# Two products of a chunked state-space scan, done in three rounded passes instead of one in full precision, with the carried state updated in place

## The chip, the cores and the metric

One core of a Trainium2 chip. The time is the device time of one execution in microseconds (us); of several runs the median is given.

## The reference

A decoder layer on 512 tokens of 1024 channels in float32: a gated feed-forward block, a mixer with two parallel branches (sliding-window attention and a Mamba-2 scan), and a second feed-forward block, each with a layer norm behind it. The change touches the scan. It goes over 4 groups of 8 heads and, in each, over 4 chunks of 128 tokens:

```
CB = jnp.einsum("bclgn,bcsgn->bcgls", Cc, Bc)
y_diag = jnp.einsum("bcgls,bcgkls,bcsgkp->bclgkp", CB, Lmat, xdt)
decay_states = jnp.exp(A_cum[..., -1:] - A_cum)
states = jnp.einsum("bclgn,bcgkl,bclgkp->bcgkpn", Bc, decay_states, xdt)
...
    return d_c[..., None, None] * h + s_c, h
...
y_off = jnp.einsum("bclgn,bcgkpn,bcgkl->bclgkp", Cc, prev, jnp.exp(A_cum))
```

`states` is the state that a chunk adds, `prev` the state carried into a chunk, and `y_off` what the carried state gives to the output.

## The kernel before

Everything is one Tile program; each engine gets its instructions in one fixed order, which a scheduler lays down ahead of time from the program's priorities and from when it expects operands to be ready. So a changed instruction also changes the order of its neighbours, on every engine.

Large products use float32 weights and activations that are split into a rounded high part and a rounded low part (`F32R`). `mm3` (L123 to L126) makes one product of two such pairs in three passes: high by high, high by low, low by high. `split_w` (L96 to L102) splits a weight block of 128x1024: ScalarE (ACT) writes the high part `wh` (L99), VectorE (DVE) subtracts it from the raw block to get `wl` (L100). `split_act` (L142 to L146) does the same for activations (L144 on ACT, L145 on DVE). A product of two plain `F32` operands is one call of `nc.tensor.matmul`; in the trace it has two records.

The scan is `ssd(g)`, a generator, for groups g = 0 to 3. For each chunk c, `lead` builds `ud` on GpSimd (POOL, L572), `decays` multiplies `ud` by a triangle on TensorE (PE, L583, L584), takes `exp` on ACT (`seg`, L586), makes `cb` (L589, L591), multiplies `seg` by it on DVE (L593), and prepares `xdt` (DVE, L595), `yx` (POOL, L597) and, for the first three chunks, `xds` = `xdt` times its decay (POOL, L601). `products` multiplies `seg` by `xdt` (L609, eight matmuls of 64 columns, two records each), then for c > 0 the carried product `CT` by `prev` (L615), and for c < 3 the state product `Bn` by `xds` (L621). DVE scales and adds the results; the new `prev` is the old one times its decay (POOL, L626) plus the state product (L627), written to the other of two buffers. After that `yx` is gated (L629), squared on ACT (L632), scaled by `rs` (DVE L633, POOL L634, DVE L635), and `turn` transposes it on PE (L642) and splits it into `uT`.

These steps are woven into the large products by `weave`: after each main step (24 passes of 512 columns on PE) it lets the generator do one step more. The mains are the input projections `z_tiles` and `conv_tile` of the next group and the output products `w_ssm_tiles` of the group before; in the last weave, `gs_tile`, whose gate `tg` and operand `m1` have one buffer each in the pool `sp`, and whose loads and stores POOL issues. The tile pool `wp` holds three raw weight blocks and four split ones; the PSUM tiles `sm` number four.

Of the kernel before, what the change touches and what calls it, by code (L numbers as in the profile page):

```python
# [9 lines left out]
F32 = mybir.dt.float32  # L10
F32R = mybir.dt.float32r
# [3 lines left out]
P = 128  # L15
# [24 lines left out]
def hybrid_layer(  # L40
# [18 lines left out]
    def sm(name="sm"):  # L59
        return psum.tile([P, 512], F32, tag="sm", name=name)  # L60
# [62 lines left out]
    def mm3(ps, lh, ll, rh, rl, start, stop):  # L123
        nc.tensor.matmul(ps, lh, rh, start=start, stop=False)  # L124
        nc.tensor.matmul(ps, lh, rl, start=False, stop=False)  # L125
        cur["mm"] = nc.tensor.matmul(ps, ll, rh, start=False, stop=stop)  # L126
# [15 lines left out]
    def split_act(dst, ps):  # L142

        a = nc.scalar.copy(dst[0], ps)  # L144
        b = nc.vector.tensor_tensor(dst[1], ps, f(dst[0]), ALU.subtract)  # L145
        return a.ins, b.ins  # L146
# [141 lines left out]
    with tc.tile_pool(name="mix", bufs=1) as mix:  # L288
# [258 lines left out]
        with tc.tile_pool(name="ssd", bufs=1) as sp:  # L547
            ysum = sp.tile([P, 8, SEQ], F32, name="ysum")

            def ssd(g):  # L550
                uT = sp.tile([P, 4, 2, SEQ], F32R, name="uT", bufs=1)
                cst["u", g] = uT
                xn, BT, CT, Bn = cst["x", g], cst["B", g], cst["C", g], cst["Bn", g]
                hs = slice(g * HPG, (g + 1) * HPG)
                normB = sp.tile([P, 512], F32, name="normB", bufs=1)
                nc.gpsimd.dma_start(normB, norm_w[0, g * 512:(g + 1) * 512].partition_broadcast(P))

                def hb(ap):
                    return ap.unsqueeze(2).broadcast_to([P, HPG, HD])

                def hv(ap):
                    return ap.rearrange("p (h d) -> p h d", h=HPG)

                st = [{} for _ in range(NT)]

                def lead(c):
                    st[c]["ud"] = []
                    for q4 in range(2):
                        ud = sp.tile([P, 2, 4, P], F32R, name="ud", bufs=2)
                        h0 = g * HPG + 4 * q4  # L570
                        for i in range(2):
                            nc.gpsimd.tensor_tensor(  # L572
                                ud[:, i], upper.unsqueeze(1).broadcast_to([P, 4, P]),
                                f(dAr[:, i, c, h0:h0 + 4]).unsqueeze(2).broadcast_to([P, 4, P]), ALU.mult)
                        st[c]["ud"].append(ud)

                def decays(c):
                    tok = slice(c * P, (c + 1) * P)
                    segs = []
                    for ud in st[c]["ud"]:  # L580
                        ps = sm()
                        udv = ud.rearrange("p i h l -> p i (h l)")
                        nc.tensor.matmul(ps, lower_r, udv[:, 0], start=True, stop=False)  # L583
                        nc.tensor.matmul(ps, lower_r, udv[:, 1], start=False, stop=True)  # L584
                        seg = sp.tile([P, 4, P], F32, name="seg", bufs=4)
                        nc.scalar.activation(seg.rearrange("p h l -> p (h l)"), ps, AF.Exp)  # L586
                        segs.append(seg)
                    pcb = sm()
                    nc.tensor.matmul(pcb[:, :P], BT[:, tok], CT[:, tok], start=True, stop=True)  # L589
                    cb = sp.tile([P, P], F32, name="cb", bufs=2)  # L590
                    nc.vector.tensor_tensor(cb, pcb[:, :P], quarter, ALU.mult)  # L591
                    for seg in segs:
                        nc.vector.tensor_tensor(seg, seg, cb.unsqueeze(1).broadcast_to([P, 4, P]), ALU.mult)  # L593
                    xdt = sp.tile([P, 512], F32, name="xdt", bufs=2)
                    nc.vector.tensor_tensor(hv(xdt), hv(xn[:, c]), hb(dth[:, c, hs]), ALU.mult)  # L595
                    yx = sp.tile([P, 512], F32, name="yx", bufs=2)
                    nc.gpsimd.tensor_tensor(hv(yx), hv(xn[:, c]), hb(dB[:, hs]), ALU.mult)  # L597
                    xds = None
                    if c + 1 < NT:
                        xds = sp.tile([P, 512], F32, name="xds", bufs=1)  # L600
                        nc.gpsimd.tensor_tensor(hv(xds), hv(xdt), hb(dec[:, 1, c, hs]), ALU.mult)  # L601
                    st[c].update(segs=segs, xdt=xdt, yx=yx, xds=xds)

                def products(c):
                    tok = slice(c * P, (c + 1) * P)
                    segs, xdt, yx, xds = (st[c][k] for k in ("segs", "xdt", "yx", "xds"))
                    py = sm()
                    for h in range(HPG):
                        nc.tensor.matmul(py[:, h * HD:(h + 1) * HD], segs[h // 4][:, h % 4], xdt[:, h * HD:(h + 1) * HD],  # L609
                                         start=True, stop=True)  # L610
                    nc.vector.tensor_tensor(yx, yx, py, ALU.add)
                    if c > 0:
                        prev = st[c]["prev"]
                        po = sm()
                        nc.tensor.matmul(po, CT[:, tok], prev, start=True, stop=True)  # L615
                        yo = sp.tile([P, 512], F32, name="yo", bufs=1)
                        nc.vector.tensor_tensor(hv(yo), hv(po), hb(dec[:, 0, c, hs]), ALU.mult)
                        nc.vector.tensor_tensor(yx, yx, yo, ALU.add)
                    if c + 1 < NT:
                        pst = sm()  # L620
                        nc.tensor.matmul(pst, Bn[:, c], xds, start=True, stop=True)  # L621
                        new = sp.tile([P, 512], F32, name="prev", bufs=2)
                        if c == 0:
                            nc.vector.tensor_copy(new, pst)
                        else:
                            nc.gpsimd.tensor_tensor(hv(new), hv(prev), hb(dec[:, 2, c, hs]), ALU.mult)  # L626
                            nc.vector.tensor_tensor(new, new, pst, ALU.add)  # L627
                        st[c + 1]["prev"] = new
                    nc.vector.tensor_tensor(yx, yx, cst.pop(("z", g, c)), ALU.mult)  # L629
                    rs = sp.tile([P, P], F32, name="rs", bufs=2)  # L630
                    sq = sp.tile([P, 512], F32, name="yo", bufs=1)
                    nc.scalar.activation(sq, yx, AF.Square, accum_out=rs[:, 0:1])  # L632
                    nc.vector.tensor_scalar(rs[:, 0:1], rs[:, 0:1], 1.0 / 512.0, 4.0 * RMS_EPS, ALU.mult, ALU.add)  # L633
                    nc.gpsimd.tensor_tensor(rs[:, 1:2], rs[:, 0:1], mhalf[:, 0:1], ALU.pow)  # L634
                    nc.vector.scalar_tensor_tensor(yx, yx, rs[:, 1:2], normB, ALU.mult, ALU.mult)  # L635

                def turn(c):
                    tok = slice(c * P, (c + 1) * P)
                    yx = st[c]["yx"]
                    ps = sm()  # L640
                    for i in range(4):
                        nc.tensor.transpose(ps[:, i * P:(i + 1) * P], yx[:, i * P:(i + 1) * P], ident)  # L642
                    split_act((uT[:, :, 0, tok], uT[:, :, 1, tok]), ps.rearrange("p (i t) -> p i t", i=4))

                lead(0)
                yield
                for c in range(NT + 1):
                    if c < NT:
                        decays(c)
                        yield  # L650
                    if c > 0:
                        turn(c - 1)
                    if c < NT:
                        products(c)
                        if c + 1 < NT:
                            lead(c + 1)
                        yield
# [15 lines left out]

            def gs_tile(j):
                ps = gemm_T(load_w(wcols(w_in, 0, 8, OFF_GS + j * P, P)), xT, range(8))
                tg = sp.tile([P, SEQ], F32, name="tg", bufs=1)
                nc.scalar.activation(tg, ps, AF.Tanh, scale=0.5)
                nc.gpsimd.dma_start(gsd[j], tg)
                m1 = sp.tile([P, SEQ], F32, name="m1", bufs=1)
                nc.gpsimd.dma_start(m1, m1d[j])  # L680
                nc.vector.scalar_tensor_tensor(ysum[:, j], tg, 1.0, ysum[:, j], ALU.add, ALU.mult)
                nc.vector.tensor_tensor(ysum[:, j], ysum[:, j], m1, ALU.add)
# [54 lines left out]
```

## Time and profile before

| what | value |
|---|---|
| median of 3 runs | 1452.49 us (1450.7 to 1454.38) |
| the profiled execution | 1453.2 us, span of its trace 1451.5 us |
| mean granted TensorE clock | 0.994 |
| PE busy | 1426.5 us, 98% of the span |
| weight loads (PEld) | 1169.7 us, 81% |
| DVE busy | 791.5 us, 55% |
| ACT busy | 482.1 us, 33% |
| POOL busy | 195.3 us, 13% |
| DMA | 106 GB/s mean over the span |

A share of busy time is a mean over stages with different loads. PE's matmuls are pipelined, so that the record of one overlaps the next one's; what a matmul holds of PE is read from the distance between records. In a line of the timeline the number in brackets is the engine's idle time just before it, and what ended it.

### The profile page before, as it was taken

What the parts mean: (1) busy time and instruction counts of PE and PEld (TensorE: products, weight loads), DVE (VectorE), ACT (ScalarE), POOL (GpSimd) and SP (SyncE); (2) the same over time, 40 slices, a digit from 0 to 9 for tenths busy, and PEclk for the clock granted to TensorE, in tenths of its full rate; (3) what the DMA queues carried; (4) which work ended last, traced back from release to release, by engine and by line L of the source; (5) the groups of instructions that cost most, each with busy time, mean ns of one, the idle gap of its engine ahead of it and who ended that gap; (6) DMA issues with size and microseconds to landing.
All of it is one profiled execution on the core that took longest, in us unless ns stands there. A gap on an engine that the chain in (4) does not pass through costs nothing. (4 is left out here: it accounts for less than half of the span.)

```text
span 1451.5 us, 17121 instructions
## 1 busy us (share of the span) xinstructions
PE 1426.5 (98%) x6700; PEld 1169.7 (81%) x6700; DVE 791.5 (55%) x1246; ACT 482.1 (33%) x789; POOL 195.3 (13%) x214
## 2 busy tenths in 40 slices
PE   8999999999999999999999999999999999999997
PEld 6888888888877777887888888878878888888885
DVE  4343343233867884358659588686574434433235
ACT  4232232121346775223444234223313322322220
POOL 1000000000000000245244154261110000000001
PEclk9999999999999999999999999999999999999999
DMA  8433333323422133641231322345735333333321
GB/s 273 121 88 102 98 90 102 99 89 105 138 81 72 45 86 108 199 119 56 80 87 59 95 73 74 95 124 161 222 110 181 95 102 95 95 102 93 97 87 58
DMA packets 195633, 154.46 MB, mean 106 GB/s; under 512 B 6532, under 2 KB 169424, under 8 KB 195552
## 3 DMA queue, kind: packets, MB, share of 16 engines
q1 hardware_dynamic: 188608, 130.17, 30.1%
q0 software_dynamic: 6944, 23.19, 5.0%
q8 instruction: 53, 0.87, 0.3%
q14 instruction: 28, 0.23, 0.0%
HBM read 140.76 MB, written 12.58 MB: 106 GB/s over the span
## 5 line engine op out<-in xcount | busy, mean ns | idle before, releaser
L100 DVE TENSOR_TENSOR wl<-raw,wh 128x1024 fp32r<-128x1024 f32 (+1 forms) x233 | 299.6, 1287 | 417.3 <-ACT wh L99 412.6
L99 ACT CAST wh<-raw 128x1024 fp32r<-128x1024 f32 (+1 forms) x233 | 244.3, 1050 | 694.4 <-issue 323.7
L124 PE MATMUL acc<-xT,wh 128*128 128x512 f32 (+2 forms) x1120 | 441.9, 395 | 0.0
L125 PE MATMUL acc<-xT,wh 128*128 128x512 f32 (+2 forms) x1120 | 434.8, 388 | 0.0
L126 PE MATMUL acc<-xT,wl 128*128 128x512 f32 (+2 forms) x1120 | 433.8, 387 | 0.0
L124 PEld LDWEIGHTS acc<-xT,wh 128*128 128x128 f32 x1120 | 210.9, 188 | 44.5 <-issue 3.2
L125 PEld LDWEIGHTS acc<-xT,wh 128*128 128x128 f32 x1120 | 210.7, 188 | 44.2 <-issue 3.3
L126 PEld LDWEIGHTS acc<-xT,wl 128*128 128x128 f32 x1120 | 210.4, 188 | 43.0 <-issue 0.2
L124 PE MATMUL dn<-wh,hT 128*128 128x512 f32 x352 | 137.2, 390 | 0.0
L125 PE MATMUL dn<-wl,hT 128*128 128x512 f32 x352 | 137.1, 390 | 0.0
L126 PE MATMUL dn<-wh,hT 128*128 128x512 f32 x352 | 136.9, 389 | 0.0
L160 POOL TENSOR_TENSOR sts<-sts,cols 128x1 f32<-128x1 f32 x12 | 11.9, 990 | 719.9 <-DVE sts L159 719.9
L572 POOL TENSOR_TENSOR ud<-upper,dAr 128x512 fp32r<-128x512 f32 x64 | 86.4, 1378 | 104.2 <-PE sm L584 104.2
L239 DVE TENSOR_TENSOR t<-t,acc 128x512 f32<-128x512 f32 x44 | 30.2, 687 | 111.6 <-PE acc L126 111.4
L125 PEld LDWEIGHTS dn<-wl,hT 128*128 128x128 f32 x352 | 66.1, 188 | 13.7
L126 PEld LDWEIGHTS dn<-wh,hT 128*128 128x128 f32 x352 | 66.1, 188 | 13.6
L124 PEld LDWEIGHTS dn<-wh,hT 128*128 128x128 f32 x352 | 66.1, 188 | 13.6
L124 PE MATMUL z<-wh,xT 128*128 128x512 f32 x128 | 51.5, 402 | 0.0
L124 PE MATMUL acc<-uT,wh 128*128 128x512 f32 x128 | 50.5, 395 | 0.0
L126 PE MATMUL z<-wh,xT 128*128 128x512 f32 x128 | 49.9, 390 | 0.0
L125 PE MATMUL z<-wl,xT 128*128 128x512 f32 x128 | 49.9, 390 | 0.0
L126 PE MATMUL acc<-uT,wl 128*128 128x512 f32 x128 | 49.9, 390 | 0.0
(212 smaller groups left out, 1691.8 us busy)
## 6 DMA issues: line engine op xcount, KB each, us to landing
raw<-in_w_in_dram SPq DMA_DIRECT2D x66, 512.0 KB, 3.7
raw<-in_ffn_w_gate_dram SPq DMA_DIRECT2D x44, 512.0 KB, 3.8
raw<-in_ffn_w_up_dram SPq DMA_DIRECT2D x44, 512.0 KB, 3.7
raw<-in_ffn_w_down_dram SPq DMA_DIRECT2D x44, 512.0 KB, 3.6
raw<-in_w_ssm_branch_dram SPq DMA_DIRECT2D x16, 512.0 KB, 3.4
raw<-in_w_attn_branch_dram SPq DMA_DIRECT2D x8, 512.0 KB, 4.1
raw<-in_w_out_dram SPq DMA_DIRECT2D x8, 512.0 KB, 4.4
r<-in_x_dram SPq DMA_DIRECT2D x8, 256.0 KB, 5.7
```

Source lines behind the costliest of these rows:

```text
L99: nc.scalar.copy(h[:, :n], raw[:, :n])
L100: nc.vector.tensor_tensor(l[:, :n], raw[:, :n], f(h[:, :n]), ALU.subtract)
L124: nc.tensor.matmul(ps, lh, rh, start=start, stop=False)
L125: nc.tensor.matmul(ps, lh, rl, start=False, stop=False)
L126: cur["mm"] = nc.tensor.matmul(ps, ll, rh, start=False, stop=stop)
L160: nc.gpsimd.tensor_tensor(mv[:, 3:4], mv[:, 2:3], mhalf[:, 0:1], ALU.pow)
L239: nc.vector.tensor_tensor(t, t, pu, ALU.mult)
L572: nc.gpsimd.tensor_tensor(ud[:, i], upper.unsqueeze(1).broadcast_to([P, 4, P]), f(dAr[:, i, c, h0:h0 + 4]).unsqueeze(2).broadcast_to([P, 4 ...
```

## The change

The carried state `prev` and the decayed inputs (now `xd`) are each split into a high and a low part (`prs`, `xds`), and so are `C` and `B` of the chunk (`csp`, `bsp`); the two products go through `mm3`. There is one buffer of `prev` for the group, and POOL's multiply and DVE's addition write it in place. The splits of `C`, `B` and `xd` are in `decays`, that of `prev` in `products`. To make room, `gs_tile` takes its two tiles from the pool `mix`, under the names `th` (two buffers) and `ct` (three buffers), which the conv tiles use too.

```diff
+                    if c > 0:
+                        csp = sp.tile([P, 2, P], F32R, name="csp", bufs=1)
+                        split_act((csp[:, 0], csp[:, 1]), CT[:, tok])
+                        st[c]["csp"] = csp
                     if c + 1 < NT:
-                        xds = sp.tile([P, 512], F32, name="xds", bufs=1)
-                        nc.gpsimd.tensor_tensor(hv(xds), hv(xdt), hb(dec[:, 1, c, hs]), ALU.mult)
+                        xd = sp.tile([P, 512], F32, name="xd", bufs=1)
+                        nc.gpsimd.tensor_tensor(hv(xd), hv(xdt), hb(dec[:, 1, c, hs]), ALU.mult)
+                        bsp = sp.tile([P, 2, P], F32R, name="bsp", bufs=1)
+                        split_act((bsp[:, 0], bsp[:, 1]), Bn[:, c])
+                        xds = sp.tile([P, 2, 512], F32R, name="xds", bufs=1)
+                        split_act((xds[:, 0], xds[:, 1]), xd)
+                        st[c]["bsp"] = bsp
...
-                        nc.tensor.matmul(po, CT[:, tok], prev, start=True, stop=True)
+                        mm3(po, csp[:, 0], csp[:, 1], prs[:, 0], prs[:, 1], True, True)
...
-                        nc.tensor.matmul(pst, Bn[:, c], xds, start=True, stop=True)
-                        new = sp.tile([P, 512], F32, name="prev", bufs=2)
+                        mm3(pst, bsp[:, 0], bsp[:, 1], xds[:, 0], xds[:, 1], True, True)
                         if c == 0:
-                            nc.vector.tensor_copy(new, pst)
+                            prev.append(sp.tile([P, 512], F32, name="prev", bufs=1))
+                            nc.vector.tensor_copy(prev[0], pst)
                         else:
-                            nc.gpsimd.tensor_tensor(hv(new), hv(prev), hb(dec[:, 2, c, hs]), ALU.mult)
-                            nc.vector.tensor_tensor(new, new, pst, ALU.add)
-                        st[c + 1]["prev"] = new
+                            nc.gpsimd.tensor_tensor(hv(prev[0]), hv(prev[0]), hb(dec[:, 2, c, hs]), ALU.mult)
+                            nc.vector.tensor_tensor(prev[0], prev[0], pst, ALU.add)
+                        prs = sp.tile([P, 2, 512], F32R, name="prs", bufs=1)
+                        split_act((prs[:, 0], prs[:, 1]), prev[0])
+                        st[c + 1]["prs"] = prs
...
-                tg = sp.tile([P, SEQ], F32, name="tg", bufs=1)
+                tg = mix.tile([P, SEQ], F32, name="th", bufs=2)
...
-                m1 = sp.tile([P, SEQ], F32, name="m1", bufs=1)
+                m1 = mix.tile([P, SEQ], F32, name="ct", bufs=3)
```

The order of PE hardly moves; where it does, it is by a few passes. Of DVE, group 1, chunk 2, from the sum `yx`+`yo` on, before:

```order
L618 TENSOR_TENSOR yx<-yx,yo 128x512
L595 TENSOR_TENSOR xdt<-xn,dth 128x512
L629 TENSOR_TENSOR yx<-yx,zs 128x512
L100 TENSOR_TENSOR wl<-raw,wh 128x1024
L633 TENSOR_SCALAR rs<-rs 128x1
L305 SCALAR_TENSOR_TENSOR ct<-acc,cols,ct 128x511
L635 SCALAR_TENSOR_TENSOR yx<-yx,rs,normB 128x512
L305 SCALAR_TENSOR_TENSOR ct<-acc,cols,ct 128x510
```

The same place in the changed kernel (its lines are numbered up to 13 higher):

```order
L628 TENSOR_TENSOR yx<-yx,yo 128x512
L145 TENSOR_TENSOR prs<-prev,prs 128x512
L642 TENSOR_TENSOR yx<-yx,zs 128x512
L145 TENSOR_TENSOR csp<-CT,csp 128x128
L145 TENSOR_TENSOR bsp<-Bn,bsp 128x128
L145 TENSOR_TENSOR xds<-xd,xds 128x512
L305 SCALAR_TENSOR_TENSOR ct<-acc,cols,ct 128x511
L646 TENSOR_SCALAR rs<-rs 128x1
L596 TENSOR_TENSOR xdt<-xn,dth 128x512
L648 SCALAR_TENSOR_TENSOR yx<-yx,rs,normB 128x512
L305 SCALAR_TENSOR_TENSOR ct<-acc,cols,ct 128x510
L100 TENSOR_TENSOR wl<-raw,wh 128x1024
```

Four subtractions have come in ahead of the second `seg` multiply of the chunk, and one weight subtraction has moved behind the scaling of `yx`.

Of DVE, group 0, chunk 1, from the scaling of chunk 0's `yx` to the second `seg`, before:

```order
L635 SCALAR_TENSOR_TENSOR yx<-yx,rs,normB 128x512
L100 TENSOR_TENSOR wl<-raw,wh 128x1024
L305 SCALAR_TENSOR_TENSOR ct<-acc,cols,ct 128x511
L591 TENSOR_TENSOR cb<-sm,quarter 128x128
L305 SCALAR_TENSOR_TENSOR ct<-acc,cols,ct 128x510
L593 TENSOR_TENSOR seg<-seg,cb 128x512
```

and in the changed kernel:

```order
L145 TENSOR_TENSOR bsp<-Bn,bsp 128x128
L145 TENSOR_TENSOR xds<-xd,xds 128x512
L648 SCALAR_TENSOR_TENSOR yx<-yx,rs,normB 128x512
L305 SCALAR_TENSOR_TENSOR ct<-acc,cols,ct 128x511
L592 TENSOR_TENSOR cb<-sm,quarter 128x128
L305 SCALAR_TENSOR_TENSOR ct<-acc,cols,ct 128x510
L594 TENSOR_TENSOR seg<-seg,cb 128x512
```

The weight subtraction between `yx` and `cb` has moved away, behind this chunk, and two new subtractions stand ahead of `yx`.

Of POOL, group 0, from `yx` of chunk 2 to `rs` of chunk 1, before:

```order
L597 TENSOR_TENSOR yx<-xn,heads 128x512
L601 TENSOR_TENSOR xds<-xdt,dec 128x512
L626 TENSOR_TENSOR prev<-prev,dec 128x512
L572 TENSOR_TENSOR ud<-upper,dAr 128x512 x4
L634 TENSOR_TENSOR rs<-rs,cols 128x1
```

and in the changed kernel:

```order
L598 TENSOR_TENSOR yx<-xn,heads 128x512
L606 TENSOR_TENSOR xd<-xdt,dec 128x512
L573 TENSOR_TENSOR ud<-upper,dAr 128x512
L637 TENSOR_TENSOR prev<-prev,dec 128x512
L573 TENSOR_TENSOR ud<-upper,dAr 128x512 x3
L647 TENSOR_TENSOR rs<-rs,cols 128x1
```

The multiply of `prev` has moved in among the four `ud`, ahead of which it stood.

## Rows read from the trace of the kernel before

**Rows 1.** Page, part 1: busy us, share of the span, instructions.

```profile
PE 1426.5 (98%) x6700; PEld 1169.7 (81%) x6700; DVE 791.5 (55%) x1246; ACT 482.1 (33%) x789; POOL 195.3 (13%) x214
```

**Rows 2.** Timeline of PE, group 1, chunks 1 and 2: start us, duration us, instruction.

```profile
760.27 0.39 PE L124 MATMUL acc<-xT,wh 128*128 128x512 f32 x1
...
760.95 0.60 PE L642 MATMUL sm<-ident,yx 128*128 128x128 f32 x4
761.39 1.90 PE L609 MATMUL sm<-xdt,seg 128*128 128x64 f32 x16
763.13 1.08 PE L615 MATMUL sm<-prev,CT 128*128 128x512 f32 x2
764.04 1.02 PE L621 MATMUL sm<-xds,Bn 128*128 128x512 f32 x2
764.50 0.80 PE L124 MATMUL acc<-xT,wh 128*128 128x512 f32 x1
...
784.22 1.90 PE L609 MATMUL sm<-xdt,seg 128*128 128x64 f32 x16
```

**Rows 3.** Timeline of PE, group 1, chunk 0.

```profile
746.25 1.84 PE L609 MATMUL sm<-xdt,seg 128*128 128x64 f32 x15
747.92 1.08 PE L621 MATMUL sm<-xds,Bn 128*128 128x512 f32 x2
748.44 0.80 PE L124 MATMUL acc<-xT,wh 128*128 128x512 f32 x1
```

**Rows 4.** Stretches: length, busy PE, PEld, DVE, ACT, POOL, granted clock, DMA.

```profile
756.00:806.00 50.00, 50.00 (x255) 40.81 (x254) 46.53 (x64) 21.52 (x36) 24.53 (x20) 1.00 0.25 74
...
676.00:686.00 10.00, 9.12 (x40) 6.06 (x39) 9.76 (x15) 3.84 (x6) 1.30 (x1) 0.83 0.17 52
```

**Rows 5.** Timeline of PE, chunks 1 and 2 of group 0, chunk 2 of group 3.

```profile
662.79 1.10 PE L609 MATMUL sm<-xdt,seg 128*128 128x64 f32 x8 [0.80 <-DVE seg L593]
...
677.78 1.10 PE L609 MATMUL sm<-xdt,seg 128*128 128x64 f32 x8 [0.54 <-DVE seg L593]
679.22 1.18 PE L609 MATMUL sm<-xdt,seg 128*128 128x64 f32 x8 [0.34 <-DVE seg L593]
680.19 2.02 PE L615 MATMUL sm<-prev,CT 128*128 128x512 f32 x2
...
968.09 2.00 PE L609 MATMUL sm<-xdt,seg 128*128 128x64 f32 x16 [1.16 <-DVE seg L593]
```

**Rows 6.** By line: duration ns (min/median/max) or busy us, mean ns | idle before.

```profile
L595 DVE TENSOR_TENSOR xdt<-xn,dth x16: 676/682/1530, 624.3 to 957.2; 128x512 f32<-128x512 f32 x16
...
L145 DVE TENSOR_TENSOR uT<-sm,uT x16: 674/679/693, 664.1 to 996.9; 128x512 fp32r<-128x512 f32 x16
...
L591 DVE TENSOR_TENSOR cb<-sm,quarter 128x128 f32<-128x128 f32 x16 | 4.5, 279 | 0.0
...
L144 ACT CAST uT<-sm 128x512 fp32r<-128x512 f32 x16 | 9.4, 585 | 3.0 <-PE sm L642 3.0
```

**Rows 7.** Timeline of DVE, groups 0 and 1.

```profile
658.35 1.94 DVE L100 TENSOR_TENSOR wl<-raw,wh 128x1024 fp32r<-128x1024 f32 x1
...
675.71 0.75 DVE L635 SCALAR_TENSOR_TENSOR yx<-yx,rs,normB 128x512 f32<-128x512 f32 x1 [2.52 <-POOL rs L634]
...
755.43 1.72 DVE L100 TENSOR_TENSOR wl<-raw,wh 128x1024 fp32r<-128x1024 f32 x1 [1.82 <-PE sm L584]
...
772.90 0.75 DVE L305 SCALAR_TENSOR_TENSOR ct<-acc,cols,ct 128x511 f32<-128x511 f32 x1 [0.20 <-ACT ct L302]
...
776.50 0.69 DVE L308 SCALAR_TENSOR_TENSOR ct<-th,ct 128x512 f32<-128x512 f32 x1 [0.76 <-ACT th L307]
777.44 2.11 DVE L100 TENSOR_TENSOR wl<-raw,wh 128x1024 fp32r<-128x1024 f32 x1 [0.24 <-ACT wh L99]
...
782.58 0.87 DVE L593 TENSOR_TENSOR seg<-seg,cb 128x512 f32<-128x512 f32 x1
```

**Rows 8.** Timeline of POOL, group 0.

```profile
670.09 5.08 POOL L572 TENSOR_TENSOR ud<-upper,dAr 128x512 fp32r<-128x512 f32 x4 [0.95 <-PE sm L584]
```

More of the change, by code (lines that the diff above doesn't have):

```diff
@@ L564, in ssd @@
                 st = [{} for _ in range(NT)]
+                prev = []
                 def lead(c):
@@ L612, in products @@
                     if c > 0:
-                        prev = st[c]["prev"]
+                        prs, csp = st[c]["prs"], st[c]["csp"]
                         po = sm()
-                        nc.tensor.matmul(po, CT[:, tok], prev, start=True, stop=True)
+                        mm3(po, csp[:, 0], csp[:, 1], prs[:, 0], prs[:, 1], True, True)
                         yo = sp.tile([P, 512], F32, name="yo", bufs=1)
@@ L619, in products @@
                     if c + 1 < NT:
+                        bsp = st[c]["bsp"]
                         pst = sm()
-                        nc.tensor.matmul(pst, Bn[:, c], xds, start=True, stop=True)
-                        new = sp.tile([P, 512], F32, name="prev", bufs=2)
+                        mm3(pst, bsp[:, 0], bsp[:, 1], xds[:, 0], xds[:, 1], True, True)
                         if c == 0:
-                            nc.vector.tensor_copy(new, pst)
-                        else:
-                            nc.gpsimd.tensor_tensor(hv(new), hv(prev), hb(dec[:, 2, c, hs]), ALU.mult)
-                            nc.vector.tensor_tensor(new, new, pst, ALU.add)
-                        st[c + 1]["prev"] = new
+                            prev.append(sp.tile([P, 512], F32, name="prev", bufs=1))
+                            nc.vector.tensor_copy(prev[0], pst)
+                        else:
+                            nc.gpsimd.tensor_tensor(hv(prev[0]), hv(prev[0]), hb(dec[:, 2, c, hs]), ALU.mult)
[3 more added lines that the diff above has]
+                        st[c + 1]["prs"] = prs
                     nc.vector.tensor_tensor(yx, yx, cst.pop(("z", g, c)), ALU.mult)
```

## The prediction

> **What bounds the kernel now.** I read the page first. TensorE (PE) is busy 1426.5 of 1451.5 us [rows 1], so what counts is how long each matmul holds PE and where PE has to wait. The chain of waits names PE matmuls nearly throughout, so I went to the stage that the change touches, the four group passes of `ssd` between about 640 and 1004 us.
>
> There I read three things. First, the price of the two matmuls that are replaced, from PE's order in time [rows 2, 3]. Matmuls overlap, so their durations are no price: the distance from one end to the next is. Three rounded passes of 512 columns start at 760.27, and the transposes behind them at 760.95: 0.227 us a pass. In chunk 1 of group 1 the last of the 16 records of L609 ends at 761.39+1.90 = 763.29, the first rounded pass behind L615 and L621 at 764.50+0.80 = 765.30: 2.01 us, less its own 0.23, is 1.78 us for the two, 0.89 each [rows 2]. In chunk 0, where L621 stands alone, 748.09 to 749.24 is 1.15, less 0.23: 0.92 us [rows 3]. A full-precision matmul thus costs four rounded passes, in two records.
>
> Second, VectorE's (DVE) load, because every new operand needs a subtraction there. From 756 to 806 us, the dense part of group 1, DVE is busy 46.53 of 50 us while PE never pauses [rows 4].
>
> Third, the places where PE does stall. Chunk 1 of group 0: L609 waits 0.80 us for `seg` [rows 5]. Chunk 2 of group 0: 0.54 us and then 0.34 us more, and L615 at 680.19 takes 2.02 us for its two records where 1.08 is usual [rows 2, 5]: the granted clock of 676 to 686 is 0.83 [rows 4], so PE fell from 2.4 to 1.2 GHz for part of it, and (1-0.83) x 10 = 1.7 us are lost. Chunk 2 of group 3: 1.16 us, with L609 itself slow after it [rows 5]. Groups 1 and 2 have no such stall.
>
> **The change part by part.**
>
> *PE.* 12 L615 and 12 L621 become three rounded passes each. Chunk 0 of each group has the state product alone and chunk 3 the carried product alone: 8 x 0.92 = 7.4 us. Chunks 1 and 2 have both: 8 x 1.78 = 14.2 us. Together 21.6 us. In their place stand 72 passes x 0.227 = 16.3 us. PE saves **5.3 us**, all of it on the path, since PE is what ends last there. Bounds: by the ends of L615 and L621 alone (764.21 and 765.06) a full matmul is 0.85 us, a saving of 24 x 0.17 = 4.1 us; at 0.92 throughout it is 24 x 0.24 = 5.8 us.
>
> *ScalarE (ACT).* It gains 24 casts of 512 columns, 0.59 us each [rows 6], and 24 of 128 columns, which are no dearer: at most 28 us over four groups. It is busy 21.52 of 50 us in the dense stretch [rows 4]. I charge nothing; if that cover went, the late item would be the weight cast `wh`, which runs several tiles ahead.
>
> *DVE.* It gains 24 subtractions of 512 columns (`xds`, `prs`) and 24 of 128 (`bsp`, `csp`). No row shows these. The nearest are `uT`, the same line with its input in PSUM, 0.68 us, never over 0.69; `xdt`, which like them reads SBUF alone, median 0.68 and at most 1.53; and `cb` at 0.28 for 128 columns [rows 6]. I take 0.68, the median, and 0.28: 1.92 us a chunk. The other end of the bound for a wide one is 1.53. The Trainium skill (SBUF — State Buffer, section "Who interferes with whom") says that a DVE instruction with two SBUF inputs and a GpSimd instruction that reads SBUF exclude each other, and that the later one blocks until the other is done. By that rule every wide subtraction that starts under a `ud` multiply pays, and the sum could come out as in the third rival, above zero; by the median it stays at the one below. The trace agrees in part: `uT` from PSUM never stretches, `xdt` does, but in fewer than half of its cases.
>
> Where this lands decides. *Group 1, chunk 1:* `bsp`, `prs`, `xds` are queued ahead of a weight subtraction before which DVE idles 1.82 us [rows 7]: 1.64 us of work in that hole, nothing on PE. *Chunk 2:* four subtractions stand between L618 and the second `seg`, 1.92 us. DVE's idle time there is 0.20+0.76+0.24 = 1.2 us [rows 7], so `seg` comes some 0.7 us later than 782.58+0.87 = 783.45. The ninth of L609's 16 records needs it, by even spacing some 0.85 us after 784.22 [rows 2]: a slack of 1.6 us. But PE comes 3 x 0.22 = 0.7 us earlier by then. That leaves 0.2 us: no stall by the medians, and I charge 0.3 us. Group 2 repeats group 1: 0.6 us for both. *Group 0, chunk 1:* `bsp` and `xds` (0.96 us) take the place of a weight subtraction of 1.94 us ahead of `cb` [rows 7], so `seg` comes about 1 us earlier, and the 0.80 us stall goes: -0.8 us. The weight subtraction is done later, for a tile that PE reaches only after the next ones. *Group 0, chunk 2:* `yx` waits 2.52 us for `rs` on GpSimd (POOL), which is queued behind four `ud` of 5.08 us together [rows 7, 8]. It still is, and the multiply of `prev` now stands among them, some 5.08/4 = 1.3 us more if it costs what a `ud` does; but the first `seg` no longer queues behind `yx`. I charge 0, bounds -2.6 (0.54+0.34 and the clock's 1.7 gone) to +1.3. *Group 3, chunk 2:* one weight subtraction (1.2 to 2 us) moves behind `seg` and 1.92 us come in, so DVE is as late as before, while PE arrives 0.5 us sooner: +0.5 us, bounds -2.9 (1.16 and a clock fall gone) to +1.9 (two wide ones at 1.53).
>
> *In place.* The POOL multiply of `prev` may now start only when the split has read it, after one cast (0.59) and one subtraction (0.68). Behind it on POOL, in groups 1 to 3, is `rs`, which waits for two more DVE additions and ACT's square of their result in any case. Hidden: 0.
>
> *Buffers.* `xd` on POOL no longer waits for the product on PE, and `m1` loads run up to three tiles ahead. PE waits for neither now, nor for the landings; so 0. The queue gets no transfer more.
>
> Sum: -5.3 + 0.6 - 0.8 + 0 + 0.5 = **-5.0 us**. The profiled execution took 1453.2 us, 1.7 us over its span, and lies 0.7 us above the median of 1452.49. From the median: **1447.5 us**. About 0.3%, 4.4 us, is what a measurement tells from no change here, so faster means under 1448.1 and slower over 1456.8.
>
> **The rivals.**
>
> *DVE gives most of it back.* A miss of 0.2 us in the slack of chunk 2 is within what one blocked subtraction (+0.85 us) costs. If groups 1 and 2 each stall about 0.9 us instead of 0.3, and one of them brings a clock fall of 1.7 us as groups 0 and 3 have it: -5.0 + 1.2 + 1.7 = -2.1, **1450.4 us**. For it speaks that DVE is at 93% in that stretch; against it that PE's earlier arrival and DVE's idle places nearly cancel.
>
> *The old stalls go.* If the new order ends the stall and the clock fall in chunk 2 of group 0 or of group 3: about 1 us and 1.7 us more than forecast, **1444.8 us**, and less if both. Against it: the causes (`rs` behind `ud`; a full DVE queue) are still there.
>
> *DVE becomes the bound, slower.* Place: the dense 50 us of each group. Six of the new subtractions fall there, three wide and three narrow. With 3.5 us free and 1.6 us of slack, PE is held in every group once a wide one averages (3.5+1.6-3 x 0.28)/3 = 1.4 us. At 1.53 us that point is passed by 3 x 0.13 = 0.4 us; if the chunks' other waits on DVE slip by as much each (four chunks, some 2 us a group) and bring a clock fall of 1.7 us: 4 x 3.7 - 5.3 = +9.5, **1462.0 us**. For it: POOL is busy 24.53 of the 50 us [rows 4], and `xdt` does reach 1.53 [rows 6]. Against it: more than half of `xdt` stays at 0.68, and a mean of 1.4 would need nearly every one blocked. (The Trainium skill's rule on the two engines, named above, is this mechanism.)
>
> *The passes are not rounded ones.* If they ran at 0.92 us, 72 x 0.92 - 21.6 = +45 us. The same helper on tiles of the same type runs at 0.227 [rows 2]: under 0.01, in with slower.
>
> **How the numbers follow.** Forecast 0.46 (0.42 of it under 1448.1), DVE gives most back 0.36, old stalls go 0.12, DVE the bound 0.06. So faster 0.42+0.12 = 0.54, same 0.04+0.36 = 0.40, slower 0.06. The range reaches from 1444.8, where the third case lies, to 1452.5, no gain left, and leaves out half of the third case, the fourth, and what of the second runs over: some 0.16 to 0.2. The likeliest case alone: 1446 to 1449.
>
> **What would show it.** Right: L124 to L126 on `sm<-prs,csp` and `sm<-xds,bsp`, 24 each, 0.227 us apart; L619 of groups 1 and 2 without a wait for `seg`, or one under 0.5 us; the 0.80 us wait of group 0 gone; new subtractions mostly near 0.68 us. Wrong: L619 waiting over 0.8 us for `seg` in groups 1 and 2, a granted clock under 0.9 in 10 us there, `prs` and `xds` with a mean over 1.2 us, or PE waiting at the carried product for `prs`.

## The result, and the profile after

The changed kernel takes 1463.89 us (median of 4 runs, 1462.84 to 1464.38), the one before 1452.53 beside it: ratio 1.0081, 95% interval 1.0068 to 1.0095. It is slower by 11.4 us, where 1447.5 us was forecast.

The page of the profiled execution (1463.48 us, span 1461.8 us), part 1, beside [rows 1]:

```profile
PE 1428.0 (98%) x6724; PEld 1178.8 (81%) x6724; DVE 812.1 (56%) x1294; ACT 501.7 (34%) x837; POOL 202.4 (14%) x214
```

Busy times tell nothing here: PE's is nearly the same although the span grew by 10.3 us. What PE waited for between 640 and 1010 us does (us in total, times, longest), first before the change, then after it:

```profile
PE sm L609 <- DVE seg L593: 2.8, 4, 1.2
PE sm L642 <- DVE yx L635: 0.6, 1, 0.6
```

```profile
PE z L124 <- DVE CT L305: 6.2, 2, 3.2
PE sm L655 <- DVE yx L648: 3.6, 5, 1.4
PE sm L619 <- DVE seg L594: 2.8, 3, 1.2
PE sm L124 <- ACT xn L326: 0.3, 1, 0.3
```

The waits grew from 3.4 to 12.9 us. Behind the longest ones PE's clock falls, which the stretches of 10 us show (the eighth number is the granted clock):

```profile
696.00:706.00 10.00, 9.46 (x38) 7.88 (x37) 10.00 (x15) 3.84 (x6) 1.49 (x1) 0.66 0.34 105
800.00:810.00 10.00, 6.80 (x27) 5.57 (x25) 6.64 (x9) 2.96 (x6) 4.06 (x5) 0.67 0.04 15
904.00:914.00 10.00, 7.01 (x37) 6.08 (x36) 8.57 (x12) 3.39 (x6) 4.05 (x3) 0.83 0.05 12
```

(1 - clock) x 10, added up over the 37 stretches from 640 to 1010 us, is 8.5 us after and 3.4 before. So +9.5 of waits, +5.1 of clock, and -3.9 of PE time (measured further down, where 5.3 was forecast) make +10.7, against the 10.3 by which the span grew.

All three stretches lie at the same place of the program, the end of chunk 2 and the start of chunk 3 of groups 0, 1 and 2. The prediction speaks of none of them, because PE did not stall there before. Group 1, before the change, in the order of time:

```profile
791.21 0.69 DVE L629 TENSOR_TENSOR yx<-yx,zs 128x512 f32<-128x512 f32 x1
792.00 0.63 ACT L632 ACTIVATE yo<-yx 128x512 f32<-128x512 f32 x1 [2.49 <-DVE yx L629]
792.99 0.55 POOL L634 TENSOR_TENSOR rs<-rs,cols 128x1 f32<-128x1 f32 x1 [6.47 <-DVE rs L633]
793.57 0.75 DVE L635 SCALAR_TENSOR_TENSOR yx<-yx,rs,normB 128x512 f32<-128x512 f32 x1 [0.66 <-POOL rs L634]
794.37 4.93 POOL L572 TENSOR_TENSOR ud<-upper,dAr 128x512 fp32r<-128x512 f32 x4 [0.84 <-PE sm L584]
795.54 1.06 ACT L99 CAST wh<-raw 128x1024 fp32r<-128x1024 f32 x1
798.33 2.06 DVE L100 TENSOR_TENSOR wl<-raw,wh 128x1024 fp32r<-128x1024 f32 x1
```

The chain gate (L629), square (L632), `rs` on POOL (L634), scaling (L635) runs through in 3 us; then come the weight cast on ACT, its subtraction on DVE and, on POOL, four `ud`, which are those of the *next group's* first chunk. The same place after the change:

```profile
794.14 0.69 DVE L642 TENSOR_TENSOR yx<-yx,zs 128x512 f32<-128x512 f32 x1
795.24 1.05 ACT L99 CAST wh<-raw 128x1024 fp32r<-128x1024 f32 x1 [2.12 <-PE acc L125]
796.20 0.63 ACT L645 ACTIVATE yo<-yx 128x512 f32<-128x512 f32 x1
796.32 1.22 DVE L100 TENSOR_TENSOR wl<-raw,wh 128x1024 fp32r<-128x1024 f32 x1 [1.29 <-ACT wh L99]
796.42 4.02 POOL L573 TENSOR_TENSOR ud<-upper,dAr 128x512 fp32r<-128x512 f32 x3 [7.47 <-PE sm L585]
797.47 0.15 DVE L646 TENSOR_SCALAR rs<-rs 128x1 f32<-128x1 f32 x1
800.41 0.54 POOL L647 TENSOR_TENSOR rs<-rs,cols 128x1 f32<-128x1 f32 x1
800.99 1.52 DVE L648 SCALAR_TENSOR_TENSOR yx<-yx,rs,normB 128x512 f32<-128x512 f32 x1 [2.52 <-POOL rs L647]
802.43 0.74 DVE L305 SCALAR_TENSOR_TENSOR CT<-acc,cols,CT 128x510 f32<-128x510 f32 x1
803.69 0.73 DVE L305 SCALAR_TENSOR_TENSOR CT<-acc,cols,CT 128x509 f32<-128x509 f32 x1
804.57 0.76 PE L124 MATMUL z<-wh,xT 128*128 128x512 f32 x1 [3.20 <-DVE CT L305]
```

On each of three engines an instruction that used to stand behind the chain stands ahead of it: a weight cast, waiting for PE, ahead of the square; its subtraction ahead of `rs` on DVE; three `ud` ahead of `rs` on POOL. (Groups 0 and 2 have the same three swaps, with four and two `ud` ahead of `rs`.) The scaling comes 6.9 us behind the gate instead of 2.4, takes 1.52 us instead of 0.75, and on DVE it stands in front of two conv steps whose PSUM bank PE wants for `z`: 3.20 us, and a granted clock of 0.67 in the 10 us around it (part of it at 1.2 instead of 2.4 GHz).

### The profile page after: what moved, and what is told of

Read it like the earlier page. It is cut to its first block, busy times and chain, and to the rows that moved or that the text cites. A ratio compares the mean times of both kernels' runs of the same rounds, so it can differ in the third digit from the quotient of the medians.

```text
span 1461.8 us, 17249 instructions
## 1 busy us (share of the span) xinstructions
PE 1428.0 (98%) x6724; PEld 1178.8 (81%) x6724; DVE 812.1 (56%) x1294; ACT 501.7 (34%) x837; POOL 202.4 (14%) x214
## 5 line engine op out<-in xcount | busy, mean ns | idle before, releaser
L100 DVE TENSOR_TENSOR wl<-raw,wh 128x1024 fp32r<-128x1024 f32 (+1 forms) x233 | 290.0, 1246 | 404.3 <-ACT wh L99 403.7
L160 POOL TENSOR_TENSOR sts<-sts,cols 128x1 f32<-128x1 f32 x12 | 11.9, 990 | 719.8 <-DVE sts L159 719.8
```

The source lines that it names most:

```text
L100: nc.vector.tensor_tensor(l[:, :n], raw[:, :n], f(h[:, :n]), ALU.subtract)
L160: nc.gpsimd.tensor_tensor(mv[:, 3:4], mv[:, 2:3], mhalf[:, 0:1], ALU.pow)
```

## The experiments

The theories: **1, queue**: the three orders above do it. **2, load**: DVE is late because it has 24 wide and 24 narrow subtractions more, and the order is a symptom. **3, contention**, stated only after e12: beside its place in the queue, the `ud` slow DVE down while both run. (In the expectations of e1 to e3, "theory 3" is another one: that POOL's multiply in place waits for the split. It does not fit e1 and e3, and e17 keeps the update in place and is fast.) All numbers below are medians against the kernel before on the same chip; waits and clock are those of 640 to 1010 us in the profiled execution, as above. That execution is not always close to the median: it took 1461.2 us in e2, 1466.2 in e6, 1461.3 in e8 and 1446.1 in e17.

| run | us | ratio, 95% interval | PE's waits | lost to the clock |
|---|---|---|---|---|
| before (1st profile) | 1452.5 | | 3.4 | 3.4 |
| after | 1463.9 | 1.0068 to 1.0095 | 12.9 | 8.5 |
| e1 | 1460.9 | 1.0041 to 1.0065 | 14.8 | 1.7 |
| e2 | 1457.1 | 1.0020 to 1.0042 | 12.7 | 5.1 |
| e3 | 1455.7 | 1.0016 to 1.0035 | 7.4 | 1.7 |
| e4 | 1459.7 | 1.0028 to 1.0060 | 6.9 | 3.4 |
| e5 | 1451.9 | 0.9991 to 1.0013 | 3.5 | 1.7 |
| e6 | 1463.4 | 1.0061 to 1.0094 | 15.0 | 6.9 |
| e7 | 1458.2 | 1.0029 to 1.0056 | 9.9 | 5.1 |
| e8 | 1464.0 | 1.0069 to 1.0097 | 15.2 | 5.1 |
| e9 | 1459.4 | 1.0036 to 1.0065 | 11.5 | 3.5 |
| e10 | 1460.5 | 1.0040 to 1.0066 | 11.6 | 5.1 |
| e11 | 1466.1 | 1.0079 to 1.0109 | 11.9 | 5.1 |
| e12 | 1455.7 | 1.0014 to 1.0033 | 9.5 | 3.4 |
| e13 | 1457.9 | 1.0026 to 1.0051 | 10.8 | 3.4 |
| e14 | 1454.1 | 1.0000 to 1.0017 | 8.8 | 1.7 |
| e15 | 1449.8 | 0.9976 to 0.9994 | 6.5 | 0 |
| e16 | 1458.0 | 1.0025 to 1.0051 | 6.8 | 1.7 |
| e17 | 1447.6 | 0.9949 to 0.9974 | 3.0 | 0 |
| e18 | 1452.3 | 0.9994 to 1.0012 | 4.4 | 0 |

**e1, e2, e3: the place of `rs` on POOL.** `issue_after` sets the order on one engine's queue and adds no wait. e1, on the changed kernel, with `cst["pow", g, c]` naming the instruction L647:

```diff
-                lead(0)
+                if g:
+                    with tc.issue_after(cst["pow", g - 1, 2].ins):
+                        lead(0)
+                else:
+                    lead(0)
```

> The changed kernel with one order fixed: on POOL the four ud multiplies for the next group's first chunk may stand only behind rs of chunk 2 of this group, as they did before the change. PE's order stays as it is, DVE's moves in a few places. Theory 1 (queue: the three stalls near 696, 805 and 908 us of the changed kernel, some 6, 7 and 4.7 us with the low clock behind them, come from rs standing behind three or four ud on POOL): 1446 to 1451 us, and no z matmul waiting over 1 us. Theory 2 (load: the new subtractions and casts make DVE late as such, and POOL's order is a symptom): no less than 1459 us, the waits of z and of the turn still there. Theory 3 (in place: POOL's multiply waiting for the split): no change, 1463 to 1465 us.

e2 adds, for c == 2, `with tc.issue_after(cst["pow", g, 1].ins): lead(c + 1)`.

> As the kernel before it in this list, and also the ud of chunk 3 only behind rs of chunk 1 in every group (groups 0 and 3 had one ud ahead of it). Theory 1: 1 to 3 us less than without this (the waits of 1.25 us at 677 us and of 1.4 us at 980 us shrink): 1444 to 1449 us. Theory 2: no difference from the kernel before it in this list.

e3 is the reverse on the kernel before: `rs` of chunk 2 is queued behind the third `ud` of the next group.

> The kernel before the change with the order of the changed one on POOL alone: rs of chunk 2 of groups 0, 1 and 2 behind three ud of the next group's first chunk. No subtraction is added and the two products stay in full precision. DVE's scaling of yx moves behind two conv steps and cb there, so it blocks less. Theory 1: slower by 3 to 12 us, 1455 to 1465 us, with waits of the turn or of seg near the end of groups 0 to 2. Theory 2 or 3: no change from before, 1451 to 1454 us.

e3 shows that this order costs 3.3 us with none of the change's work. It is not POOL's order alone: in e3 the scheduler also put DVE's scaling behind two conv steps. But e1 won back 3.0 us where 13 to 18 were expected. In its trace (group 1, POOL, DVE, PE) `rs` is early and yet the time is lost again:

```profile
799.64 0.55 POOL L647 TENSOR_TENSOR rs<-rs,cols 128x1 f32<-128x1 f32 x1 [8.73 <-DVE rs L646]
800.15 5.38 POOL L573 TENSOR_TENSOR ud<-upper,dAr 128x512 fp32r<-128x512 f32 x4
800.22 1.52 DVE L648 SCALAR_TENSOR_TENSOR yx<-yx,rs,normB 128x512 f32<-128x512 f32 x1 [0.47 <-POOL rs L647]
805.44 0.47 PE L124 MATMUL z<-wh,xT 128*128 128x512 f32 x1 [1.45 <-DVE CT L305]
```

The `ud` now start 0.07 us ahead of the scaling that `rs` has released, and the scaling doubles. Before, the `ud` came 0.8 us after the scaling's start. It was the first sign of theory 3. e2 is 3.8 us under e1.

**e4, e5, e6: the gate's buffers.** e4 is the `gs_tile` part of the change on the kernel before, and nothing else.

> The kernel before the change with the two tiles of the gate taken from the pool of the conv tiles, and nothing else of the change. All theories: no change, 1451 to 1454 us; a rival in which the new buffers matter (loads that come early, DMA issues standing between POOL's multiplies) would show over 2 us either way.

The theories expected no change; the rival named beside them came true, and it costs 7.3 us (95% interval of the ratio 1.0028 to 1.0060; its trace shows 3.5 us more waits between 640 and 1010 us, and the rest is not located). POOL and DVE in group 2 (L680 is the issue of a load of `m1`):

```profile
892.79 0.15 DVE L633 TENSOR_SCALAR rs<-rs 128x1 f32<-128x1 f32 x1 [0.85 <-ACT yo L632]
893.02 0.58 POOL L680 DMA_DIRECT2D ct<-m1d  x1 [10.04 <-PE sm L583]
893.62 0.57 POOL L634 TENSOR_TENSOR rs<-rs,cols 128x1 f32<-128x1 f32 x1
894.16 4.03 POOL L572 TENSOR_TENSOR ud<-upper,dAr 128x512 fp32r<-128x512 f32 x4
894.22 4.52 DVE L635 SCALAR_TENSOR_TENSOR yx<-yx,rs,normB 128x512 f32<-128x512 f32 x1
```

The loads may now be issued as soon as a conv tile is free, so the scheduler puts three issues among POOL's multiplies of group 2, 60 us and more ahead of their use. One stands before `rs`; `rs` is 0.6 us late, so the `ud` start just ahead of the scaling, which is held up for the whole of them: 4.52 us. PE then waits 2.4 us for `CT`. e5 leaves the buffers and moves the issues:

```diff
-                nc.gpsimd.dma_start(m1, m1d[j])
+                with tc.issue_after(cst["pow", 2, 2].ins):
+                    nc.gpsimd.dma_start(m1, m1d[j])
```

> The kernel before the change with the gate's two tiles in the conv tiles' pool, as in the run of that change alone (1459.7 us), but the loads of m1 are issued on POOL only behind rs of chunk 2 of group 2. Theory 1 (queue: the early m1 issues wait on POOL for a conv buffer and hold up rs, ud and yx behind them; that is where the 7 us came from): 1451 to 1454 us, no wait of z or seg near 882 and 900 us. Rival (the buffers themselves are dear, whoever issues when): 1457 to 1461 us.

The 7 us are gone: the buffers are free, the place of the issues was not. e6 puts the same lines into e1:

> The changed kernel with two orders fixed on POOL: rs of chunk 2 ahead of the next group's ud (1460.9 us so far), and the m1 loads behind rs of chunk 2 of group 2. Theory 1: 2 to 5 us less than with rs alone, 1456 to 1459 us; the z wait of group 2 shrinks and that of group 1 stays. Theory 2 (load: the new subtractions make DVE late as such): 1459 to 1462 us.

It came out 2.5 us over e1 instead of under. Its waits are e1's (15.0 and 14.8 us); it lost 6.9 us to the clock where e1 lost 1.7. So that term moves by some 5 us between kernels with equal waits, and e6's own executions reach from 1459.5 to 1466.2 us. A step from one run to the next is therefore laid to an order only where the trace shows the wait that came or went.

**e7 to e10: the weight splits.** e7 adds to e6 that a weight split goes behind the square and `rs` that were current two weight tiles earlier (`cst` keeps the last of each):

```diff
+        hist.append((cst.get("sq"), cst.get("rs")))
+        with ExitStack() as s:
+            for i in hist[-1 - 2] if len(hist) > 2 else ():
+                if i:
+                    s.enter_context(tc.issue_after(i.ins))
+            nc.scalar.copy(h[:, :n], raw[:, :n])
+            nc.vector.tensor_tensor(l[:, :n], raw[:, :n], f(h[:, :n]), ALU.subtract)
```

> As the kernel before it in this list, and in addition a weight cast (ACT) and weight subtraction (DVE) stand behind the square and rs of the products that were traced two weight tiles earlier, so that no early weight split stands in front of the chain square, rs, scaling of yx. Theory 1 (three queues: a 0.6 us subtraction made the square miss its place, and the weight cast on ACT, the weight subtraction on DVE and ud on POOL went ahead of the chain): 1449 to 1454 us, z waits under 1 us in groups 1 and 2. Theory 2 (load): 1457 us or more, since nothing of the work is taken away.

```profile
PE acc L131 <- DVE wl L105: 3.6, 1, 3.6
PE sm L623 <- DVE seg L598: 2.7, 3, 1.6
PE acc L129 <- ACT wh L104: 2.0, 2, 1.8
PE sm L659 <- DVE yx L652: 1.6, 3, 0.6
```

PE's waits in e7: none is left at `z`, with all of the change's work in place. The time is lost elsewhere, by weights that now come late themselves. e8 also puts the update of `prev` and the four new splits behind the chain:

> As the kernel before it in this list, and in addition the update of prev is written behind the scaling of yx, and the four new splits stand behind the last square on ACT and the last rs on DVE. Theory 1: the whole saving of the passes is left, 1445 to 1450 us. Theory 2: 1456 us or more. A rival within theory 1: prs comes too late for the next carried product and PE waits there, 1452 to 1458 us.

A miss: its `z` waits 8.4 us for `CT`. Its trace shows what sets that: the subtraction of `prs`, put behind the chain, now meets the `ud`, and the conv steps stand behind it (group 2):

```profile
897.20 4.99 DVE L156 TENSOR_TENSOR prs<-prev,prs 128x512 fp32r<-128x512 f32 x1
897.60 4.02 POOL L583 TENSOR_TENSOR ud<-upper,dAr 128x512 fp32r<-128x512 f32 x4
905.10 0.77 PE L129 MATMUL z<-wh,xT 128*128 128x512 f32 x1 [5.36 <-DVE CT L315]
```

e9 holds back one weight split only, the one that had slipped (the list above filled for c == 2 and g < 3, four tiles back), together with e6's two orders; e10 does so without them.

> The changed kernel, all of its work kept, with the order of three queues as before the change at the three places where it slipped (chunk 2 of groups 0, 1, 2): one weight cast on ACT behind the square and one weight subtraction on DVE behind rs, rs on POOL ahead of the next group's ud; m1 loads behind rs of group 2. The earlier weaker version held back more weight splits and paid 6.5 us for late weights in group 0; this one holds back one. Theory 1 (three queues): all three events (6.4, 6.7 and 4.9 us) go to under 1 us each, 1446 to 1451 us. Theory 2 (load): 1455 us or more.

> The changed kernel with the weight cast and weight subtraction held behind the square and rs as in the kernel before it in this list, but rs on POOL left where the change put it, behind the next group's ud. Theory 1 in its full form (each queue does harm): between the changed kernel and the kernel before it in this list, 1453 to 1460 us, with the scaling of yx still waiting for rs over 1.5 us. If POOL's place alone does it: 1462 to 1465 us. If the weight split alone does it: 1446 to 1451 us.

e9 is a miss too, 1459.4 us; e10, 1460.5 us, lies between e9 and the changed kernel, as theory 1 had it, but above its range. Even with all three orders put back (e9), the `ud` now right behind `rs`, the time does not come back. That looked like a point for theory 2. But e9's longest wait, 3.56 us for `seg` in group 0, stands behind a scaling, a conv step and two `seg` multiplies that took about 1.5 us each beside those `ud`.

**e11, e12.** e11 is e9 with both products in full precision, the splits being made and left unused; e12 is e9 with e2's order.

> As the first kernel of this list, with all splits made but the two products left in full precision, as before the change: the load without the saving. The difference to the first kernel of this list is the price of the passes on PE: by the term of the prediction 5.3 us more. Theory 1: 1452 to 1456 us. If the new work on DVE costs by itself, with every queue in order: over 1457 us.

> As the first kernel of this list, and rs of chunk 1 on POOL ahead of all ud of chunk 3, which concerns groups 0 and 3. Theory 1: 0.5 to 2 us less than the first kernel of this list (the 1.25 us wait of the turn at 677 us goes, the seg waits of 1.4 and 1.3 us near 980 us shrink to 0.5 each, a wait of 1 us for xds may come): 1445 to 1450 us. Theory 2: no difference.

e11 lies 6.7 us over e9, where the saving on PE was put at 5.3; e12 is 3.7 us under e9, more than expected. Both lie above the ranges that theory 1 gave for them.

**e13 to e16: the `ud` out of the way.** e13 is e1 with `cst["pow", g - 1, 3]`: the next group's `ud` go behind `rs` of chunk 3, ahead of a stretch in which POOL idles for 16 to 25 us. e14 adds the orders of e2 and e5, e15 that of e9; e16 is e13's line in the kernel before.

> The changed kernel with one order fixed on POOL: the four ud for the next group's first chunk stand behind rs of chunk 3 of this group, some 15 us later than in the changed kernel and still well before PE needs them; nothing else is moved by hand, and weight casts stay ahead of the square. Theory 3 (contention with ud, beside the queue): the stretch of chunk 3 in groups 0 to 2 is free of ud, the scaling of yx takes 0.75 us there, stalls of 17.7 us in the three stretches fall under 6: 1449 to 1455 us. Theory 2 (load): no better than with rs ahead of ud alone, 1458 to 1461 us.

> As the kernel before it in this list, and also rs of chunk 1 ahead of all ud of chunk 3 in groups 0 and 3, and the m1 loads behind rs of chunk 2 of group 2. Theory 3: 1 to 4 us less than the kernel before it in this list, 1446 to 1452 us. Theory 2: no difference, 1456 to 1460 us.

> As the kernel before it in this list, and one weight split held behind the square and rs of chunk 2 in groups 0 to 2, as before the change. Theory 3 with the three queues: the most that order can give back, 1445 to 1449 us, faster than before the change. Theory 2: 1454 us or more. A rival: the held weight split comes late in group 0 (4 us, as in two earlier kernels): 1449 to 1453 us.

> The kernel before the change with the next group's ud behind rs of chunk 3 on POOL. Nothing stalls in those stretches before the change, so all theories: 1451 to 1454 us, no change. If it gains over 2 us, part of what the three kernels above win is not the change's own.

The ladder goes down, but each step ends above the range that theory 3 gave: 1457.9, 1454.1, 1449.8. And e16, where no theory expected a change, is slower by 5.2 us; its PE waits 3.9 us for the scaling at three turns. What happens there is seen in e15 as well (e15, group 1, POOL, DVE and PE):

```profile
807.22 4.47 POOL L577 TENSOR_TENSOR ud<-upper,dAr 128x512 fp32r<-128x512 f32 x3
807.29 1.52 DVE L654 SCALAR_TENSOR_TENSOR yx<-yx,rs,normB 128x512 f32<-128x512 f32 x1 [1.39 <-POOL rs L653]
808.96 0.63 PE L661 MATMUL sm<-ident,yx 128*128 128x128 f32 x4 [1.37 <-DVE yx L654]
```

Again the `ud` start together with the scaling, this time one that the turn on PE waits for.

**e17, e18: the `ud` behind the scaling.** POOL's load of `normB` waits for the last scaling of the group before; behind it the `ud` (and `xd` of chunk 1) can collide with no scaling. e17 is e15 with

```diff
-                nc.gpsimd.dma_start(normB, ...
+                nrm = nc.gpsimd.dma_start(normB, ...
...
-                    with tc.issue_after(cst["pow", g - 1, 3].ins):
+                    with tc.issue_after(nrm.ins):
                         lead(0)
```

> As the best version so far (1449.8 us), but on POOL the next group's ud, and the decayed inputs xd of its chunk 1, stand behind the load of normB, which waits for the scaling of yx of chunk 3; all work of the change is kept. Theory 3 (contention and queue): the scaling takes 0.75 us there, the three stalls at the turn of chunk 3 go: 1445 to 1447.5 us, which is the time that the prediction gave. Theory 2 (load): 1449 to 1451 us, the turn still waits.

> The kernel before the change with the next group's ud behind the load of normB on POOL. By theory 3 no stall of its own: 1451 to 1454 us, and so the difference to the kernel before it in this list, 5 to 7 us, is what the passes are worth when no queue slips. If it is under 1450 us, the order has a gain of its own that the change does not share.

```profile
806.08 0.75 DVE L657 SCALAR_TENSOR_TENSOR yx<-yx,rs,normB 128x512 f32<-128x512 f32 x1 [0.73 <-POOL rs L656]
806.98 0.63 PE L664 MATMUL sm<-ident,yx 128*128 128x128 f32 x4
807.13 0.60 POOL L560 DMA_DIRECT2D normB<-in_ssm_norm_w_dram  x1 [1.08 <-DVE yx L657]
807.75 4.03 POOL L577 TENSOR_TENSOR ud<-upper,dAr 128x512 fp32r<-128x512 f32 x4
```

The scaling takes 0.75 us and PE does not wait. e17's page and PE's waits:

```profile
PE 1419.5 (98%) x6724; PEld 1172.0 (81%) x6724; DVE 825.9 (57%) x1294; ACT 501.4 (35%) x837; POOL 198.7 (14%) x214
```

```profile
PE sm L626 <- DVE seg L598: 1.8, 3, 1.1
PE sm L130 <- DVE xds L150: 1.0, 1, 1.0
PE sm L664 <- DVE yx L657: 0.2, 1, 0.2
```

1447.6 us, faster than before by 0.4% (0.9949 to 0.9974), with all of the change's arithmetic and a DVE busier than in the slow kernel (825.9 against 812.1 us). The place of the `ud` alone, in the kernel before (e18), changes nothing; e17's other orders were not tried there. So theory 2 falls: nothing was taken from DVE and 16.3 us came back. What the change cost is order (theory 1) and what then runs side by side (theory 3), and the two hang together, since an order decides what meets what. That 1447.6 us is the time that was forecast is in part luck: the passes save less than forecast, and e17 has orders that neither kernel had.

## Why the prediction was wrong

- **PE saves 5.3 us: right in kind, but too large.** The passes are rounded. Group 1, chunk 2, the first and the last of the six, between their neighbours:

```profile
786.64 1.90 PE L619 MATMUL sm<-xdt,seg 128*128 128x64 f32 x16
788.34 0.48 PE L124 MATMUL sm<-prs,csp 128*128 128x512 f32 x1
...
789.58 0.40 PE L126 MATMUL sm<-xds,bsp 128*128 128x512 f32 x1
789.82 0.39 PE L124 MATMUL acc<-xT,wh 128*128 128x512 f32 x1
```

  Five steps in 1.24 us, 0.25 each with the first one's start in it. By the prediction's own measure, from the end of L619 to the end of the first pass behind, the six take 1.67 us where the two full products took 2.01 [rows 2]; in chunk 0 three take 0.99 where one took 1.15 [rows 3]. That is some 0.33 and 0.16 us saved, where the sum had 0.42 and 0.24: 8 of each make 3.9 us, under the lower bound of 4.1. The sum left out that the first pass of such a group takes 0.32 us to the next one. e17 against e18, both without a fall of the clock: 4.7 us between the medians, but e17's profile also has 1.4 us less of waits.
- **The subtractions: right.** Minimum, median and maximum of `prs` in ns:

```profile
L145 DVE TENSOR_TENSOR prs<-prev,prs x12: 679/687/693, 655.2 to 988.6; 128x512 fp32r<-128x512 f32 x12
```

  None of the 24 wide ones was blocked (`xds`: at most 695); the narrow ones averaged 0.42 us instead of 0.28, since four of them took 1.07 to 1.14 us, each beside a POOL multiply. The third rival, at 1462.0 us, gave nearly the time that was measured, but by luck, through a mechanism that did not happen in the changed kernel: it had the *new* wide subtractions blocked by POOL. The rule of the Trainium skill (SBUF — State Buffer, "Who interferes with whom") was met by an *old* instruction, the scaling of `yx`: 0.75 us alone, 1.52 with one `ud` ahead, 4.52 beside four (e4). In e8, by another order, a new one met it: `prs`, 4.99 us.
- **The stalls priced: the 0.6 and 0.5 us that were charged were not the trouble.** In chunks 1 and 2 of groups 1 and 2 PE does not wait for `seg` (0.3 us had been charged for chunk 2 of each group). In group 0, chunk 1, the 0.80 us are gone, as forecast. Group 0, chunk 2 has the turn waiting 1.09 us and keeps its clock (1.00 from 676 to 686 us); group 3, chunk 2 waits 1.21 and 1.06 us instead of 1.16 and a clock fall [rows 5].
- **"So 0" for the buffers: wrong.** It asked whether PE waits for the loads. The price is on the queue that issues them: 7.3 us by themselves (e4), 0 with the issues held back (e5). In the changed kernel, holding them back won nothing that can be told (e6 against e1).
- **"I charge nothing" for ACT, with the weight cast as the late item: wrong.** The cast was not late, it was early: it went ahead of the square and made that wait for PE.
- **The step that failed** is the reading of the order, and with it a sum that has no term for the end of chunk 2 and the start of chunk 3 of groups 0 to 2, where 8.2 of PE's 12.9 us of waits and all of the 8.5 us lost to the clock lie, against 3.9 us that the passes save. The order was read at the places where PE stalled before, and the new work was weighed against slack there. The stretch that went bad had no stall, and what hit it was for the most part no added work (one `prs` of 0.69 us stands ahead of the gate there), but three swaps on three queues, each with an instruction that waits or runs long. They stood in the order of the changed kernel. The pieces of order shown ahead of the prediction are of other places: the one of DVE in group 1 ends at the conv steps of `ct`, where the scaling stood between the same two steps before and after; the stretch that went bad comes one chunk later, at the conv steps of `CT`. For groups 1 to 3 the prediction says that `rs` stands behind the multiply of `prev`, which was harmless; that in chunk 2 of groups 0 to 2 it had come behind the next group's `ud` was not seen.

What stays open: which of e17's orders could be left out, what they would do in the kernel before, and whether the `prs` ahead of the gate is what made the scheduler swap the three.

## What to carry to other kernels

Where a scheduler lays down the order, compare the two orders of every queue for swaps with an instruction that waits or runs long, everywhere, and first on the chain that crosses most engines (gate, square, `rs`, scaling, turn): in this kernel the scaling came 6.9 us behind the gate instead of 2.4, by what went ahead of it. A tile moved to another pool moves the issue of its load too; price the queue that it lands in. If a change does what it should on its bound engine and the time still rises, hold the work and restore the order before blaming the load, and look in the trace at what the restored order runs side by side.

## What was not expected of the hardware

- How long the same instruction takes depends on where a POOL multiply starts: the scaling of `yx`, 128x512 with two operands in SBUF, took 0.75 or 1.52 us, once 3.52 beside three `ud` (e10) and once 4.52 beside four that ran undisturbed in 4.03 us (e4). Putting `ud` right behind the instruction that releases the scaling made them meet in e1, e15 and e16.
- The granted clock lost up to 8.5 us in this part in the slow kernels and nothing in e15, e17 and e18; e1 and e6, with equal waits, differ by 5.2 us in it.
